# Output weights gated, summed and split beside the first attention units instead of in the output stage

## The chip, the core and the metric

The kernel runs on one core of one Trainium2 chip. The metric is the device time of one execution in microseconds, as a median over several runs. The engines are TensorE (PE, matmuls; PEld is its weight load), VectorE (DVE), ScalarE (ACT), GpSimd (POOL) and SyncE (SP), which here issues nearly all of the DMAs. Each engine works through its own instructions in order. On-chip memory is SBUF; matmuls write to PSUM; DRAM is reached by DMA.

## The reference

One layer of a hybrid backbone: 2048 latent tokens and 256 context tokens of width 1024. After a modulated RMS norm, one input projection feeds a bidirectional gated delta-rule scan (branch A, 4 heads) and a windowed grouped-query attention (branch B, 8 heads of 64, window 128, all context keys, a sink). Both go through their own projections and are merged by gates, then comes the output projection with a gated residual:

```python
def _merge(ya, yb, ga, gb, w_proj_a, w_proj_b, w_out):
    y = jax.nn.sigmoid(ga) * (ya @ w_proj_a) + jax.nn.sigmoid(gb) * (yb @ w_proj_b)
    return y @ w_out
...
    x = x + gate[:, None] * _merge(ya, yb, ga, gb, w_proj_a, w_proj_b, w_out)
```

`gate` is one vector of 1024 numbers, a factor for each output column, known early in the kernel. All data is fp32.

## The kernel before

**Numbers.** Each fp32 operand of a large matmul is split into a high half (a cast to a rounded fp32 format) and a low half (the rest), and each product is three matmuls: high by high, high by low, low by high. The cast is mostly on ACT, the subtraction for the low half on DVE or POOL.

**Stages.** The modulation and the norm; the input projection; the delta-rule scan over chunks; attention in 32 units (16 blocks of 128 tokens, 2 key heads); the two branch projections with the merge (`project`, lines 1280 to 1310); the output stage (from line 1372). A scheduler orders the first stages. It lets TensorE run gate products of the input projection (24 matmuls each, `rps`, lines 586 to 588) and later the projections' matmuls (`pps`, lines 1293 to 1295) between those of the scan and of the attention units, as fillers. The tokens are in four groups `gi` of 512, worked in the order 1, 2, 0, 3.

**Attention.** A unit has four heads' scores (`sc`, lines 971 to 974), their maximum and exponential (`pr`, DVE line 978, ACT line 980), a scaling (POOL line 988), transposes on TensorE (`pt`, line 1002), the split of the transposed probabilities (`ph` on ACT, line 1004, and `pl` on DVE, line 1006) and the products with the values (`av`, lines 1008 and 1009). `avt` then carries the result to DRAM (ACT line 1012, DVE line 1013, POOL line 1014, a DMA). Scores are two units ahead of the products. Twelve filler matmuls stand in most of the first units.

**Merge.** For group `gi` and column block `m` of 128, `project` loads the gates `ta` and `tb`, multiplies both projections by them, adds them on DVE or POOL and stores the sum to the DRAM tensor `ysp`. The last group's column blocks 6 and 7 are summed late, inside the output stage (`late_sum`, lines 1312 to 1324).

**Output stage.** The product of each 256 tokens by 1024 columns is made by seven block products instead of eight (Strassen-Winograd), `u` = 0 to 7 being the 256-token units. On the weights' side there are the blocks B11, B21, B22 and the sums T3 = B22 - B12, T2 = T3 + B11, T1 = B22 - T2, T4 = B21 - T2; on the activations' side A11, A12, A22, S1 to S4. One block product is 12 matmuls of 128x512 (line 1539 high by high, 1540 with the weights' low half, 1541 with the activations' low half `al`). The order of the products: each of the first two units' seven in pairs (P1 of u=0 and u=1, P2 of both, P3, P7, P6, P5, P4), then unit by unit. The four blocks of `w_out` are loaded from ACT's queue (line 1394) during the last group's projection and split there and in the first products: casts on ACT, the low halves and sums as 128x2048 instructions on DVE and POOL (lines 1411, 1444, 1446, 1578, 1583). The activations are read from `ysp` (line 1406). `his` (ACT, line 1421) and `los` (DVE, POOL for P4, line 1425) split them, five and four products ahead. `store` (lines 1489 to 1494) multiplies each finished quadrant by `gate` (line 1491), adds the residual's `x` (line 1492) and sends it out. The order of DVE, ACT, POOL and TensorE in this stage is written out by hand.

## Time and profile before

| | |
|---|---|
| time, median of 3 runs | 1974.95 us (1970.47 to 1976.83) |
| profiled execution | 1977.22 us |
| its span | 1975.5 us |
| granted TensorE clock, mean | 0.994 |
| busy: PE / DVE / ACT / POOL | 96% / 77% / 41% / 35% |

The profile is of one execution. A row of a timeline has its start, its duration, the engine with the line of the kernel, the operation, and the tiles written and read; in brackets stands how long the engine was idle before, and what ended that. A row of groups ends with the count, the busy time, the mean duration in ns and the idle time before. "SPq" is a DMA issue on SyncE, and its duration is that of the issue. Line numbers in the rows are those of the kernel before.

### The profile page before, as it was taken

To read this page: it belongs to the slowest core of one execution; us is meant where nothing else is said; L and a number is where in the kernel's file an instruction comes from. 1 tells how busy PE (TensorE), PEld (TensorE's weight loads), DVE (VectorE), ACT (ScalarE), POOL (GpSimd) and SP (SyncE) were. 2 spreads that over 40 slices of the span, in tenths; PEclk is the share of its full clock that TensorE was granted. 3 is DMA by queue.
4 is the path that set the end of the run, shared out by engine and by line. 5 is a ranking of instruction groups with operands and counts; after the bars stand their busy time and mean duration, and the time that the engine had idled before them with its cause. 6 is when DMAs were issued, how large, how long until landed. Compare 5 with 4: busy or idle time off the path is not lost. (4 is left out here: it accounts for less than half of the span.)

```text
span 1975.5 us, 32093 instructions
## 1 busy us (share of the span) xinstructions
PE 1902.6 (96%) x10931; PEld 1596.3 (81%) x10931; DVE 1512.4 (77%) x2873; ACT 815.6 (41%) x2011; POOL 701.3 (35%) x772
## 2 busy tenths in 40 slices
PE   6899999989999899999999999999999999999998
PEld 3888888788998787887888888888878887877786
DVE  7888766678776899999778776535787868757888
ACT  6865545544443322211122233324765646532321
POOL 2652111235543201104222334323555443422675
PEclk9999999999999999999999999999999999999999
DMA  7453226765546633537887777765455645355453
GB/s 267 161 154 93 87 89 161 190 166 166 152 146 169 178 108 115 151 96 208 230 251 219 224 227 228 197 182 188 136 182 178 195 150 173 113 190 175 144 171 134
DMA packets 387640, 333.13 MB, mean 169 GB/s; under 512 B 83928, under 2 KB 307472, under 8 KB 386836
## 3 DMA queue, kind: packets, MB, share of 16 engines
q1 hardware_dynamic: 352132, 288.58, 50.4%
q10 hardware_dynamic: 35344, 42.49, 6.2%
q8 instruction: 87, 1.43, 0.3%
q14 instruction: 77, 0.63, 0.1%
HBM read 220.28 MB, written 109.13 MB: 167 GB/s over the span
## 5 line engine op out<-in xcount | busy, mean ns | idle before, releaser
L586 PE MATMUL rps<-hh,wh 128*128 128x512 f32 x768 | 308.5, 402 | 6.5 <-DVE rt L880 5.4
L588 PE MATMUL rps<-hh,wl 128*128 128x512 f32 x768 | 307.7, 401 | 0.2 <-DVE wl L244 0.2
L587 PE MATMUL rps<-hl,wh 128*128 128x512 f32 x768 | 306.3, 399 | 0.0
L625 DVE SCALAR_TENSOR_TENSOR cacc<-y,cw,cacc 128x512 f32<-128x512 f32 (+1 forms) x224 | 163.5, 752 | 23.3 <-ACT cacc L623 21.0
L586 PEld LDWEIGHTS rps<-hh,wh 128*128 128x128 f32 x768 | 144.9, 189 | 41.8 <-DVE rt L880 6.3
L588 PE MATMUL lps<-hh,wl 128*128 128x512 f32 (+1 forms) x448 | 171.6, 383 | 1.7 <-DVE wl L244 1.7
L586 PE MATMUL lps<-hh,wh 128*128 128x512 f32 (+1 forms) x448 | 172.0, 384 | 0.8 <-POOL wh L243 0.6
L588 PEld LDWEIGHTS rps<-hh,wl 128*128 128x128 f32 x768 | 144.8, 188 | 32.6 <-DVE wl L244 0.3
L587 PEld LDWEIGHTS rps<-hl,wh 128*128 128x128 f32 x768 | 144.8, 189 | 32.5
L587 PE MATMUL lps<-hl,wh 128*128 128x512 f32 (+1 forms) x448 | 171.0, 382 | 0.0
L1006 DVE TENSOR_TENSOR pl<-pt,ph 128x512 fp32r<-128x512 f32 x156 | 105.6, 686 | 42.3 <-ACT ph L1004 41.4
L1004 ACT CAST ph<-pt 128x512 fp32r<-128x512 f32 x156 | 90.8, 585 | 107.8 <-PE pt L1002 72.8
L878 ACT ACTIVATE rt<-rps 128x512 f32<-128x512 f32 x96 | 57.2, 596 | 181.5 <-PE rps L588 157.9
L978 DVE CUSTOM_DVE_ANT_0 pr<-sc,band,sk 128x640 f32<-128x640 f32 (+1 forms) x128 | 106.7, 862 | 19.8 <-PE sc L974 12.1
L988 POOL TENSOR_SCALAR pr<-pr,sm 128x640 f32<-128x640 f32 (+1 forms) x128 | 101.4, 813 | 54.7 <-DVE sm L986 39.9
L809 DVE TENSOR_TENSOR btmp<-N 128x62 f32<-128x62 f32 (+30 forms) x124 | 117.4, 946 | 3.1
L811 DVE TENSOR_TENSOR N<-N,btmp 128x62 f32<-128x62 f32 (+30 forms) x124 | 116.1, 936 | 3.0
L980 ACT ACTIVATE pr<-pr,sm 128x640 f32<-128x640 f32 (+1 forms) x128 | 104.1, 815 | 24.1 <-DVE sm L978 24.1
L1293 PE MATMUL pps<-yh,wph 128*128 128x512 f32 x256 | 105.7, 415 | 2.4 <-DVE tb L1304 2.1
L244 DVE TENSOR_TENSOR wl<-wr,wh 128x512 fp32r<-128x512 f32 x120 | 91.6, 775 | 20.2 <-POOL wh L243 17.9
L243 POOL TENSOR_SCALAR wh<-wr 128x512 fp32r<-128x512 f32 x72 | 49.5, 700 | 156.4 <-PE lps L587 85.2
L1295 PE MATMUL pps<-yh,wpl 128*128 128x512 f32 x256 | 101.6, 398 | 0.9 <-POOL wpl L1255 0.9
(382 smaller groups left out, 5028.2 us busy)
## 6 DMA issues: line engine op xcount, KB each, us to landing
wr<-in_w_in_dram SPq DMA_DIRECT2D x120, 256.0 KB
kw<-Ksp SPq DMA_DIRECT2D x28, 384.0 KB
x<-vsp SPq DMA_DIRECT2D x36, 256.0 KB
k<-ksp SPq DMA_DIRECT2D x34, 256.0 KB
kT<-kTsp SPq DMA_DIRECT2D x34, 256.0 KB
wm<-in_w_mod_dram SPq DMA_DIRECT2D x16, 512.0 KB
xt<-in_x_dram SPq DMA_DIRECT2D x16, 512.0 KB
dtl<-Dsp SPq DMA_DIRECT2D x32, 256.0 KB
```

What stands on the lines that cost most here:

```text
L586: T.matmul(ps, lhsT=wh[:, k], rhs=xh[:, k], start=k == 0, stop=False)
L587: T.matmul(ps, lhsT=wh[:, k], rhs=xl[:, k], start=False, stop=False)
L588: T.matmul(ps, lhsT=wl[:, k], rhs=xh[:, k], start=False, stop=k == kt - 1)
L625: V.scalar_tensor_tensor(a, y[:, t:t + n], cw[:, m, t:t + 1], a, op0=ALU.mult, op1=ALU.add)
L809: V.tensor_tensor(tv, A[:, m + 1:, m].unsqueeze(2).to_broadcast([h1 + n, r, m]), A[:, m, 0:m].unsqueeze(1).to_broadcast([h1 + n, r, m]), o ...
L811: V.tensor_tensor(A[:, m + 1:, 0:m], A[:, m + 1:, 0:m], tv, op=ALU.add)
L978: V.tensor_tensor_reduce(s_, ps[:, o:768], band[:, b0:b0 + W + 256], -0.125, sk[:, 1, hd:hd + 1], ALU.add, ALU.min, sm[:, h, 1:2])
L980: S.activation(s_, s_, AF.Exp, scale=-1.0, bias=sm[:, h, 1:2], accum_out=sm[:, h, 2:3])
L988: G.tensor_scalar(p[:, h, :W + 256], p[:, h, :W + 256], sm[:, h, 3:4], 1.0, op0=ALU.mult, op1=ALU.mult)
L1006: V.tensor_tensor(pl, pt, f32(ph), op=ALU.subtract)
L1293: T.matmul(ps, lhsT=wh[:, k, ms], rhs=hs[k], start=k == 0, stop=False)
L1295: T.matmul(ps, lhsT=wl[:, k, ms], rhs=hs[k], start=False, stop=k == 3)
```

## The change

The blocks of `w_out` leave the output stage. A generator, `out_weights`, works on them in sixteen pieces of 128x512: for each quarter `k` of the rows it loads the four blocks' pieces, multiplies them by the columns of `gate` (on DVE for k = 0 and 1, on POOL for 2 and 3), forms the four sums on POOL, casts all seven to the high half on ACT, subtracts for the low half on DVE, and stores both halves to one of seven new DRAM tensors `wsp` (0.5 MB a store, 28 stores). It has seven steps for each quarter. The first two quarters are called ahead of unit 0's products, the last two by two steps after each unit, and their instructions are placed behind the unit's last ones on ACT, DVE, POOL and SP. Pieces (`wb`) and halves (`whl`) have two buffers each.

The output stage then loads the seven finished matrices, high and low halves together (2.1 MB each, `load_w`), and no longer touches weights. The loads stand in SP's queue: three of them between the last group's gate loads, four behind the last of these, between loads of `x`. Since the gate is in the weights, `store` only adds: `gather` adds a product, straight from PSUM where it can, to the `x` tile. There are ten `x` tiles instead of four. `ysp` is laid out so that 128 tokens of all columns lie together, and one DMA reads both column halves (`yA1`, `yA2`). The gate's broadcast tile in the output stage is gone.

```diff
-    ysp = many("ysp", 4, [128, KT, 512])
+    ysp = many("ysp", 4, [4, 128, KT, 128])
+    wsp = {nm: dscr(f"w{nm}", [128, 2, 4, 512]) for nm in ("B11", "B21", "B22", "T3", "T2", "T1", "T4")}
...
+    def out_weights(pool):
+        gates_ = [pool.tile([128, 512], F32, name="gbc", tag="tb") for _ in range(2)]
+        for j, t in enumerate(gates_):
+            dma(t, gsp[:, j * 512:j * 512 + 512].to_broadcast([128, 512]))
+        for k in range(4):
+            b = {}
+            for pair in (("B22", "B12"), ("B11", "B21")):
+                t = pool.tile([128, 2, 512], F32, name="wb", tag="ybh")
+                for n, nm in enumerate(pair):
+                    i, j = int(nm[1]) - 1, int(nm[2]) - 1
+                    b[nm] = t[:, n]
+                    dma(b[nm], ins["w_out"][0, i * 512 + k * 128:i * 512 + k * 128 + 128, j * 512:j * 512 + 512])
+            yield
+            def gated(nm):
+                (V if k < 2 else G).tensor_tensor(b[nm], b[nm], gates_[int(nm[2]) - 1], op=ALU.mult)
+            def put(nm, src):
+                t = pool.tile([128, 2, 512], F32R, name="whl", tag="ybl")
+                S.copy(t[:, 0], b[src])
+                V.tensor_tensor(t[:, 1], b[src], f32(t[:, 0]), op=ALU.subtract)
+                dma(wsp[nm][:, :, k], f32(t))
+            gated("B22")
+            gated("B12")
+            put("B22", "B22")
+            yield
+            G.tensor_tensor(b["B12"], b["B22"], b["B12"], op=ALU.subtract)
+            gated("B11")
+            put("T3", "B12")
+            yield
...
+            G.tensor_tensor(b["B21"], b["B21"], b["B11"], op=ALU.subtract)
+            put("T1", "B22")
+            put("T4", "B21")
+            yield
...
+        for _ in range(14):
+            next(beside)
         for i, (n, kv) in enumerate(units):
             if i + AHEAD < len(units):
                 start(i + AHEAD)
-            weighted(n, kv, qs[n], pr.pop(i))
+            ended = weighted(n, kv, qs[n], pr.pop(i))
+            with ExitStack() as paced_by:
+                for e in ended:
+                    paced_by.enter_context(tc.issue_after(e.ins))
+                next(beside, None)
+                next(beside, None)
...
+            dma(ysp[gi][:, :, m].rearrange("o p c -> p o c"), us[0].rearrange("p (o c) -> p o c", c=128))
...
         def load_w(nm):
-            i, j = int(nm[1]) - 1, int(nm[2]) - 1
-            adma(B[nm], ins["w_out"][0, i * 512:i * 512 + 512, j * 512:j * 512 + 512].rearrange("(k p) c -> p k c", p=128))
+            t = home.get(nm, hr).tile([128, 2, 4, 512], F32R, name=nm)
+            dma(f32(t), wsp[nm])
+            hi[nm], lo[nm] = t[:, 0], t[:, 1]
...
+            for m, jobs in enumerate(([(load_w, "B11")], [(load_quad, 0, "A1"), (load_quad, 1, "A1")], [(load_w, "B21")],
+                                      [(load_quad, 0, "A2"), (load_quad, 1, "A2")], [(load_w, "B22")])):
+                with tc.issue_after(last["t", m].ins):
+                    for f, *a in jobs:
+                        f(*a)
...
-                S.copy(hi["B11"], B["B11"])
-                split_lo("B11", V)
...
-                S.copy(hi["B22"], B["B22"])
-                V.tensor_tensor(B["B12"], B["B22"], B["B12"], op=ALU.subtract)
...
-            split_lo("B22", G)
-            split_lo("T3", G, "B12")
...
-        def store(u, q, t, eng):
-            xr, dst, gate, j = X.pop((u, q))
-            eng.tensor_tensor(t, t, gate, op=ALU.mult)
-            (V if u == 7 else G).tensor_tensor(xr, t, xr, op=ALU.add)
+        def gather(eng, u, q, t):
+            xr = X[u, q][0]
+            eng.tensor_tensor(xr, t, xr, op=ALU.add)
+        def store(u, q, ps):
+            gather(V, u, q, ps)
+            xr, dst, j = X[u, q]
             dma(dst, xr)
-            load_x(j + 4)
+            load_x(j + 10)
...
             elif nm == "P5":
-                h2 = wq.tile([128, 2, 512], F32, name="hold2", tag="wl")
-                V.tensor_tensor(h2[:, 0], ps, held[u][:, 0], op=ALU.add)
-                V.tensor_tensor(h2[:, 1], ps, held[u][:, 1], op=ALU.add)
-                V.tensor_tensor(h2[:, 0], R[u, "P3"], h2[:, 0], op=ALU.add)
-                store(u, "11", h2[:, 1], V)
-                store(u, "01", h2[:, 0], V)
...
+                store(u, "11", ps)
+                store(u, "01", ps)
             elif nm == "P4":
-                V.tensor_tensor(held[u][:, 1], ps, held[u][:, 1], op=ALU.add)
-                store(u, "10", held[u][:, 1], gp)
+                store(u, "10", ps)
...
+                for j in range(2):
+                    load_x(j)
+                load_w("T3")
+                for j in range(2, 6):
+                    load_x(j)
+                load_w("T2")
+                load_w("T1")
+                for j in range(6, 10):
+                    load_x(j)
+                load_w("T4")
```

How the instructions stand. First SP's queue at the scan's end, where the first attention units' loads are issued. `sza` and `yasp` are the scan's last gated outputs, `wr` the weights of the gate products, `kw`, `kc`, `qT` and `vw` the attention's loads. Before:

```order
L239 DMA wr<-in_w_in_dram 128x4x128 x2
L1125 DMA yasp_138<-sza 128x4x128
L956 DMA kw<-Ksp 128x2x384 x4
L1125 DMA yasp_135<-sza 128x4x128
L239 DMA wr<-in_w_in_dram 128x4x128 x2
L929 DMA kc<-Ksp 128x2x256 x2
L931 DMA vc<-Vsp 128x2x256
```

And now:

```order
L948 DMA gbc<-gsp 128x512 x2
L956 DMA wb<-in_w_out_dram 128x512 x4
L966 DMA wB_137<-whl 256x1x512
L240 DMA wr<-in_w_in_dram 128x4x128
L1179 DMA yasp_142<-sza 128x4x128
L240 DMA wr<-in_w_in_dram 128x4x128
L966 DMA wT_138<-whl 256x1x512
L966 DMA wB_135<-whl 256x1x512
L930 DMA kc<-Ksp 128x2x256 x2
L932 DMA vc<-Vsp 128x2x256
```

The pieces' loads and three of their stores now stand ahead of the attention's first loads, and two more stand behind these.

Second, DVE's line from the scan's end to the first scores, after the change (`L960` multiplies by the gate, `L965` makes a low half, `L1025` is line 978 before). Before, the instructions of lines 960 and 965 are not there:

```order
L1262 TENSOR_TENSOR oa_13330<-ops,oa_13330 128x512
L960 TENSOR_TENSOR wb<-wb,gbc 128x512
L1170 TENSOR_TENSOR oa_13330<-oa_13330,fss 128x512
L960 TENSOR_TENSOR wb<-wb,gbc 128x512
L965 TENSOR_TENSOR whl<-wb,whl 128x512
L960 TENSOR_TENSOR wb<-wb,gbc 128x512
L245 TENSOR_TENSOR wl<-wr,wh 128x512
L1178 SCALAR_TENSOR_TENSOR sza<-fps,gw,sza 128x512
L960 TENSOR_TENSOR wb<-wb,gbc 128x512
L245 TENSOR_TENSOR wl<-wr,wh 128x512
L965 TENSOR_TENSOR whl<-wb,whl 128x512 x4
```

Two more of the first quarter's low halves stand behind the first two scores' maxima, and the second quarter's eleven instructions between these and unit 0's end. The last two quarters' fourteen low halves are spread over units 1 to 7, two behind each unit's `avt` or a little later.

Third, SP's queue from the end of the last group's gate loads (`ta`, `tb`) to the first stores of output, after the change. Before, the weights' loads stood in ACT's queue instead, four of 1 MB:

```order
L1375 DMA ta<-gasp_126 128x512
L1513 DMA xr<-in_x_dram 128x512 x2
L1443 DMA T_19662<-wT_138 128x4096
L1513 DMA xr<-in_x_dram 128x512 x4
L1443 DMA T_19672<-wT_139 128x4096
L1443 DMA T_19674<-wT_140 128x4096
L1513 DMA xr<-in_x_dram 128x512 x4
L1443 DMA T_19684<-wT_141 128x4096
L1380 DMA ysp_134<-ta 128x4x128 x2
L1523 DMA out_dram<-xr 128x512 x2
```

The last four matrices now wait in this queue behind everything that the merge loads, and the last two `ysp` stores and the first output stores wait behind them.

More of the change, by code (lines that the diff above doesn't have):

```diff
@@ L1308, in project @@
                 continue
-            (V if gi == 3 else G).tensor_tensor(us[0], us[0], us[1], op=ALU.add)
-            dma(ysp[gi][:, m], us[0])
+            last["sum"] = (V if gi == 3 else G).tensor_tensor(us[0], us[0], us[1], op=ALU.add)
+            dma(ysp[gi][:, :, m].rearrange("o p c -> p o c"), us[0].rearrange("p (o c) -> p o c", c=128))
         return left
+    late_loads = []
     def late_sum(gi, m, us):
@@ L1330, in _hybrid @@
     psum_phase("right", sc=2, pt=2, av=1)
+    pj_ = tc.tile_pool(name="proj", bufs=2, side="right", reuse_waits="tile")
+    pj = pj_.__enter__()
     al_ = tc.tile_pool(name="attl", bufs=2, reuse_waits="tile")
@@ L1334, in _hybrid @@
     ar = ar_.__enter__()
-    attention(al, ar, [4 * gi + j for gi in (1, 2, 0, 3) for j in range(4)], att_consts(al))
+    attention(al, ar, [4 * gi + j for gi in (1, 2, 0, 3) for j in range(4)], att_consts(al), out_weights(pj))
     gates(list(range(BESIDE, 22)), (1, 0))
     wp, last = {}, {}
-    with tc.tile_pool(name="proj", bufs=2, reuse_waits="tile") as pj:
+    if True:
         raw = [pj.tile([128, 2, 512], F32, name="wpr", tag=tag) for tag in ("ybh", "ybl")]
@@ L1473, in s1 @@
             Y[u, "S1"] = Y[u, "A11"]
-        R, held, early = {}, {}, {}
+        with tc.high_priority(tc.cur_priority - p_last), \
+                tc.manual_schedule(engines={EN.DVE, EN.Activation, EN.Pool}):
+            for m, jobs in enumerate(([(load_w, "B11")], [(load_quad, 0, "A1"), (load_quad, 1, "A1")], [(load_w, "B21")],
[3 more added lines that the diff above has]
+                        f(*a)
+            with tc.issue_after(last["yh", 3].ins), tc.issue_after(last["yl", 3].ins):
+                for k in range(2):
+                    his(k)
+                    los(k)
+                s3(0, V)
+                s2(0, V)
+                s3(1, V)
+                s2(1, V)
+        for k in range(2, NP):
+            pair(k)
+        R, held = {}, {}
         outs = [(u, q) for u, nm in seq for q in {"P2": ["00"], "P5": ["11", "01"], "P4": ["10"]}.get(nm, [])]
@@ L1502, in outputs @@
                 S.copy(held[u][:, 0], ps)
+                gather(G, u, "00", held[u][:, 0])
             elif nm == "P2":
-                og = ev.tile([128, 512], F32, name="og", tag="rt")
-                V.tensor_tensor(og, ps, held[u][:, 0], op=ALU.add)
-                if u < 2:
-                    early[u] = og, G
-                else:
-                    store(u, "00", og, gp)
+                store(u, "00", ps)
+            elif nm == "P3":
+                gather(V, u, "01", ps)
             elif nm == "P6":
@@ L1540, in product @@
                 T.matmul(ps, lhsT=h[:, j], rhs=wl[:, j], start=False, stop=False)
-                end = T.matmul(ps, lhsT=l[:, j], rhs=wh[:, j], start=False, stop=j == 3)
-            return end
+                T.matmul(ps, lhsT=l[:, j], rhs=wh[:, j], start=False, stop=j == 3)
         with tc.manual_schedule(engines={EN.DVE, EN.Activation, EN.Pool, EN.PE}):
@@ L1610, in _hybrid @@
                 if k < len(seq):
-                    end = product(k)
-                if k == 3:
-                    with tc.issue_after(end.ins):
-                        dma(gbc, gsp.to_broadcast([128, D]))
-                        for j in range(4):
-                            load_x(j)
+                    product(k)
                 if k:
```

142 lines of the change are left out of this document (47 added, 95 removed).

## The prediction

> **What bounds the kernel now.** I read the page's busy shares first, then the chain, then the table by stretches, then TensorE's waits in the stretches that the change touches.
>
> ```profile
> span 1975.5 us, 32093 instructions
> PE 1902.6 (96%) x10931; PEld 1596.3 (81%) x10931; DVE 1512.4 (77%) x2873; ACT 815.6 (41%) x2011; POOL 701.3 (35%) x772
> DVE 0%; issue 0%
> ```
>
> TensorE is busy 96% of the span, so only its 73 us without work, and work that it does slowly, can be won. The chain of waits is no help: it holds five pieces at the very end. So each stage is read by itself.
>
> ```profile
> 1801.00:1875.00 74.00, 65.98 (x274) 51.64 (x273) 65.86 (x63) 20.21 (x30) 40.42 (x22) 0.98 0.46 143
> 1875.00:1968.00 93.00, 92.88 (x402) 74.94 (x400) 79.59 (x89) 19.29 (x35) 65.44 (x41) 1.00 0.48 156
> 1300.00:1350.00 50.00, 49.06 (x233) 40.05 (x233) 15.39 (x32) 10.98 (x32) 9.52 (x19) 1.00 0.75 231
> 1350.00:1400.00 50.00, 49.92 (x281) 42.91 (x280) 35.96 (x84) 30.70 (x69) 21.34 (x27) 1.00 0.44 140
> 1400.00:1450.00 50.00, 49.02 (x273) 40.35 (x272) 39.89 (x87) 37.19 (x79) 26.08 (x28) 1.00 0.49 150
> ```
>
> Columns: stretch, its length, then busy time of PE, PEld, DVE, ACT and POOL, granted clock, DMA share, GB/s. The output products run from 1801 to 1968. Their second part is dense: 402 matmuls in 93.00 us, 0.2313 us each. At that pace the 274 of the first part need 63.4 us; they took 74.0. So 10.6 us are lost there, and in the second part none. The attention's opening units (1350 to 1450) have TensorE full, with DVE free for 14.0 and 10.1 us of 50.
>
> TensorE's waits between 1801 and 1875 name the loser:
>
> ```profile
> PE P L1541 <- DVE al L1425: 7.3, 4, 3.1
> PE P L1541 <- POOL al L1425: 0.7, 1, 0.7
> ```
>
> Total, times, longest. All are waits for `al`, the low half of an activation. Why it is late, by the timelines of DVE, POOL and PE:
>
> ```profile
> 1798.45 2.29 DVE L1411 TENSOR_TENSOR B21l<-B,B21h 128x2048 fp32r<-128x2048 f32 x1 [1.99 <-PE pps L1294]
> 1800.66 9.76 DVE L1425 TENSOR_TENSOR al<-yA,ah 128x512 fp32r<-128x512 f32 x1
> 1812.26 0.68 DVE L1425 TENSOR_TENSOR al<-yA,ah 128x512 fp32r<-128x512 f32 x1
> ...
> 1798.71 6.59 POOL L1411 TENSOR_TENSOR B22l<-B,B22h 128x2048 fp32r<-128x2048 f32 x1 [41.01 <-PE pps L1295]
> 1805.26 4.61 POOL L1411 TENSOR_TENSOR T3l<-B,B12h 128x2048 fp32r<-128x2048 f32 x1
> ...
> 1810.48 0.50 PE L1541 MATMUL P<-B21h,al 128*128 128x512 f32 x1 [3.10 <-DVE al L1425]
> 1812.02 0.63 PE L1539 MATMUL P<-B21h,ah 128*128 128x512 f32 x1
> 1812.45 0.63 PE L1540 MATMUL P<-B21l,ah 128*128 128x512 f32 x1
> ...
> 1833.55 0.50 PE L1541 MATMUL P<-T2h,al 128*128 128x512 f32 x1 [1.56 <-DVE al L1425]
> ```
>
> A 0.68 us subtraction took 9.76 us while POOL split two weight matrices; it ended with them. TensorE stood 3.10 us, and afterwards ran for a while at 0.43 us a matmul (1812.02 to 1812.45), which is why 8.0 us of waits cost 10.6. The other stalls have the weights' wide DVE instructions ahead of them in line, 2.29 us each (first row).
>
> **The change part by part.**
>
> *Output stage.* It takes all weight work off this stage: both POOL splits, DVE's nine 2.29 us instructions (20.6 us), ACT's seven wide casts, and the gate's multiplications. DVE's 65.86 us in the first part fall by about 9.1 (the stretched subtraction) and five to six wide ones, to 45 of 74. What remains there is work like that of the second part, where TensorE loses nothing. I take 10 of the 10.6 us; at least 6 should go, since the 3.10 us stall with its slow matmuls and the 1.56 us one both stand directly behind such work.
>
> *The end.*
>
> ```profile
> 1967.48 0.40 PE L1541 MATMUL P<-T4h,al 128*128 128x512 f32 x1
> 1971.81 0.69 DVE L1527 TENSOR_TENSOR xr<-hold,xr 128x512 f32<-128x512 f32 x1
> 1972.53 0.33 SPq L1528 DMA_DIRECT2D out_dram<-xr  x1
> ```
>
> From the last matmul's start to the span's end there are 8.0 us, in which DVE works off its line. Now one addition straight from PSUM follows the last product: 0.40 + 0.69 + about 0.2 of handing over + the last store's 2.97 (1972.53 to 1975.5) is 4.3. Gain 3.5, between 3 and 4.
>
> *Loads of the split weights.* High and low halves in fp32 are 2.1 MB a matrix, against 1.05 MB and only four matrices before. In SP's line the last four wait behind the final project loads:
>
> ```profile
> 1798.96 0.90 SPq L1318 DMA_DIRECT2D tb<-gbsp  x2
> ...
> 1801.21 0.39 PE L1539 MATMUL P<-B11h,ah 128*128 128x512 f32 x1
> ```
>
> These were out by 1799.86. From there: 1.05 MB of those loads, ten input rows of 0.26 MB and four matrices, 12.05 MB. The first product starts at 1801.21; at 2.8 us for each (12 matmuls), T4's, the thirteenth, starts at 1834.8. That asks for 345 GB/s. The traffic view of 1763 to 1782, where the weights come in today:
>
> ```profile
> GB/s 362 78 0 0 69 52 198 392 405 410 401 375 342 317 303 309 381 384 375 401 401 367 371 375 388 388 388 392 375 388 388 379 348 341 346 396 401 406 392 276
> DMA packets 4366, 6.20 MB, mean 327 GB/s; under 512 B 192, under 2 KB 1728, under 8 KB 4365
> ```
>
> At its mean of 327 the last weights are 1.9 us late; at 303, the lowest slice of the busy part, 5; at 375 or more, not at all. I take 2, bounds 0 and 5. For the earlier three matrices I add nothing: the 51 us from 1750 to 1801 moved this,
>
> ```profile
> DMA packets 7736, 11.82 MB, mean 232 GB/s; under 512 B 536, under 2 KB 2449, under 8 KB 7735
> ```
>
> and must now move some 15 MB (2.1 more of weights, 1.3 more of activations), which is 299 GB/s. The Trainium skill gives, in "DMA: Bandwidth & Descriptors", section Specifications, about 358 GB/s as a core's share of HBM; this trace has slices up to 410, so the measurement decides, and by the page's figure as an estimate this term would be 0 instead of 2.
>
> *The weight work's new place.* Sixteen pieces are multiplied (eight on DVE, eight on POOL), 16 sums on POOL, 28 casts on ACT, 28 subtractions on DVE, 28 stores of 0.5 MB. The nearest rows, by groups, 1350 to 1450:
>
> ```profile
> L244 DVE TENSOR_TENSOR wl<-wr,wh 128x512 fp32r<-128x512 f32 x4 | 3.2, 827 | 0.1
> L1275 DVE TENSOR_TENSOR yl<-yr,yh 128x512 fp32r<-128x512 f32 x2 | 1.3, 689 | 0.0
> L1004 ACT CAST ph<-pt 128x512 fp32r<-128x512 f32 x41 | 23.6, 584 | 15.9 <-PE pt L1002 10.1 <-PE av L1008 5.4
> L1255 POOL TENSOR_TENSOR wpl<-wpr,wph 128x512 fp32r<-128x512 f32 x4 | 5.1, 1289 | 2.4 <-ACT wph L1254 2.4
> ```
>
> So DVE gets 36 x 0.69 = 25 us, ACT 28 x 0.58 = 16, POOL 24 x 1.29 = 31. By the order of the instructions, of DVE's 36 the eleven of the first quarter stand at the scan's end and the first scores. They fit: DVE is idle 34.6 us of 1300 to 1350, and what they delay there (the last `sza` and the gate's splits) has fillers before it. Next:
>
> (a) The first scores come one gate product later on TensorE, and that product's boundary loses its cover. Such a boundary today:
>
> ```profile
> 1331.91 0.50 PE L586 MATMUL rps<-hh,wh 128*128 128x512 f32 x1 [0.69 <-ACT rt L878]
> ```
>
> With the slower matmul behind it, 1 us.
>
> (b) The second quarter's eleven stand between unit 0's scores and its end, in some 22 us (1350 to 1372) with 28% of DVE free, 6.2 us. They need 7.6: 1.4 late. If each of the four POOL sums beside them also holds one up by its 1.29, 5.2 more. Bounds 0 (DVE was free before 1350) and 7; I take 3, since DVE is handed these by a store's end too (two buffers only).
>
> (c) The last two quarters add two DVE, two ACT and 2.3 POOL instructions to each of units 1 to 7. The units' ends on DVE:
>
> ```profile
> 1372.91 0.68 DVE L1013 TENSOR_TENSOR avt<-av,avt 64x512 f32<-64x512 f32 x1
> ...
> 1449.88 0.68 DVE L1013 TENSOR_TENSOR avt<-av,avt 64x512 f32<-64x512 f32 x1
> ```
>
> Seven units lie between, 11.0 us each; DVE's 10.1 free of 50 are 2.2 a unit, against 1.4 needed. That fits, barely; ACT (37.19 of 50, plus 5.6) and POOL (26.08, plus 14) fit too. If each of the two meets a POOL instruction for its full 1.29, 4.0 stand against 2.2, and each unit ends 1.8 later: 13. TensorE has nothing else to do then, as the fillers are placed by units. Between 0 and 13 the nearest row is L244, a subtraction beside POOL's work that rose only from 0.69 to 0.83; that fits into the free time. I take 2 for queueing.
>
> The stores put qT, kw and szb loads behind themselves in SP's line; these are ahead by two units, 22 us, against some 3 for a store: nothing, unless the units themselves slip. The first projection's weights move behind the last pieces; gate products stand in front of them: nothing, up to 4.
>
> The sum: -10 - 3.5 + 2 + 1 + 3 + 2 = -5.5. From the profiled execution (1977.22, 1.7 around its span) that is 1971.7; it lay 2.3 above the median of the runs shown, from which it is 1969.5. I predict 1970.
>
> **The rivals.**
>
> *A, the opening hides everything.* DVE's idle 34.6 us ahead of 1350 take so much that units 0 to 7 lose nothing but (a), and the loads hold 375 GB/s: -13.5 + 1, 1962.5. For it: free time on all three engines. Against it: DVE's line is in order, and what is free is free in scraps.
>
> *B, slower: DVE's line in the opening units.* Place: from unit 0's `pl` to unit 7's. Price: POOL's long instructions hold each of DVE's added ones as the 9.76 us row was held: 1 + 6 + 12, with 2 for the loads, against 13.5: +7.5, 1982.5. It decides from the point at which a unit's added DVE time passes 2.2 us, that is, when its two instructions are held 0.4 us each on average, as by one POOL instruction in three. The Trainium skill says in "SBUF — State Buffer", section Who interferes with whom, that a DVE instruction with two SBUF inputs and a GpSimd instruction that reads SBUF hold each other for the whole instruction, while a DVE instruction with at most one SBUF input isn't held outside the two-port modes. All 36 added ones have two; attention's `pl` reads PSUM and isn't held itself. By that rule B would be the forecast; the 9.76 us row agrees with it. Against B: L244's 827 ns beside POOL's instructions.
>
> *C, no change: the loads.* T3 to T4 and the fourth matrix come at 303 GB/s and in turn: 5 and again some 3 at the third or sixth product, and the opening's 6: -13.5 + 14, 1975.5. The wait by `al` becomes a wait by a load. For it: twice the bytes. Against it: slices of 375 to 410.
>
> **How the numbers follow.** A measurement of this kernel can tell about 0.3%, 5.9 us, from no change: faster is below 1969.0, slower above 1980.9. Forecast 0.42, its own range 1965 to 1975, half of it faster; A 0.20, all faster; B 0.22, of which 0.18 slower; C 0.16, of which 0.05 slower. That is faster 0.21 + 0.20 = 0.41, slower 0.23, the same 0.36. A's and B's outer halves left out, the range is 1962 to 1984.
>
> **What would show it.** Right: no wait for `al` over 1 us between the first product and the second part, the first 274 output matmuls within 66 us; one DVE addition behind the last matmul and 4.3 us to the end; DVE's subtractions of the pieces near 0.7 to 0.9 us; the opening units ending 6 us late against the scan. For B: those subtractions at 1.3 us and above, and TensorE waiting for `ph`, `pl` or scores in units 0 to 7. For C: TensorE or ACT waiting for a DMA of T2, T1 or T4. Wrong altogether: if the scan or the gates' products ahead of the attention lose time, or if the stalls between 1801 and 1875 stay although the weight work is gone.

## The result, and the profile after

The changed kernel takes 2001.49 us (median of 6 runs, 1995.14 to 2005.34) where the kernel before takes 1975.37 beside it: 1.0132 of it, 95% interval 1.0112 to 1.0153. It is 26 us slower, and outside the range that was given. Its profiled execution has a span of 2003.0 us.

The page of the kernel after, its first lines:

```profile
span 2003.0 us, 32226 instructions
PE 1913.3 (96%) x10931; PEld 1607.0 (80%) x10931; DVE 1489.6 (74%) x2880; ACT 819.4 (41%) x2032; POOL 698.3 (35%) x781
```

TensorE has the same 10931 matmuls, and they occupy it 11 us longer. Of these, 3 us lie ahead of the scan's end; the others are slower matmuls around the waits (granted clock 0.95 up to unit 0's end and 0.98 from there to unit 7's, 1.00 in both before). The rest of the 27.5 us is waiting. To place them I read four moments in each kernel's timelines: the last transposes of the scan (`fps` on PE), the ends of unit 0 and unit 7 (`avt` on DVE), the first output product and the last matmul (`P` on PE). All are starts of rows. In us:

| | scan's end to unit 0 | unit 0 to 7 | scan's end to first output product | first to last output matmul | last matmul's start to the end |
|---|---|---|---|---|---|
| before | 48.4 | 77.0 | 476.7 | 166.3 | 8.0 |
| after | 63.7 | 87.9 | 502.4 | 167.8 | 4.1 |

So 25.7 us are lost between the scan's end and the first output product, the output stage gains nothing (1.5 us more), and the end gains 3.9. The remaining 4.2 us lie ahead of the scan's end; that moment stood between 1324.0 and 1332.9 in the executions of all the kernels below, and I draw nothing from it.

**The opening.** First unit 0. ACT's and DVE's waits from 1328 to 1392 in the kernel after (total, times, longest):

```profile
ACT whl L964 <- DMA wT<-whl: 9.8, 3, 4.7
ACT whl L964 <- DMA wB<-whl: 2.7, 2, 1.4
DVE whl L965 <- ACT whl L964: 13.5, 5, 5.3
```

ACT's cast waits until the store of two casts earlier has left its buffer, and DVE stands in line behind that cast. One such case by the timelines of SP, ACT, DVE and PE:

```profile
1345.10 0.53 SPq L966 DMA_DIRECT2D wT<-whl  x1
...
1354.10 0.62 ACT L964 CAST whl<-wb 128x512 fp32r<-128x512 f32 x1 [4.15 <-DMA wT<-whl]
...
1354.75 0.69 DVE L965 TENSOR_TENSOR whl<-wb,whl 128x512 fp32r<-128x512 f32 x1 [2.50 <-ACT whl L964]
1359.17 0.69 DVE L965 TENSOR_TENSOR whl<-wb,whl 128x512 fp32r<-128x512 f32 x1 [3.72 <-ACT whl L964]
1359.78 0.88 DVE L1025 CUSTOM_DVE_ANT_0 pr<-sc,band,sk 128x640 f32<-128x640 f32 x1
...
1360.72 0.44 PE L1018 MATMUL sc<-kw,qT 128*128 128x384 f32 x1 [2.85 <-DVE sm L1025]
```

A store issued at 1345.10 had not released its buffer before 1354.10, nine us later. The scores' maximum (L1025) stands behind two low halves, and TensorE waits 2.85 us for it. The second of these low halves waited 3.72 us for a cast that stood on ACT behind an exponential (L1027, 1357.71), so stores are not all of it.

Then the later units. First the stretches 1392 to 1467 of the kernel after and 1373 to 1450 of the kernel before (columns as in the prediction), then groups on DVE in them:

```profile
1392.00:1467.00 75.00, 64.66 (x349) 53.41 (x349) 70.10 (x122) 51.07 (x110) 56.44 (x52) 0.97 0.75 243
...
L965 DVE TENSOR_TENSOR whl<-wb,whl 128x512 fp32r<-128x512 f32 x12 | 13.7, 1153 | 1.9 <-ACT whl L964 1.2 <-DMA vw<-Vsp 0.6
L1029 DVE TENSOR_TENSOR es<-sm,sk 128x4 f32<-128x4 f32 x6 | 8.1, 1345 | 0.0
L1031 DVE TENSOR_TENSOR es<-es,sm 128x4 f32<-128x4 f32 x6 | 3.5, 575 | 0.2 <-ACT es L1030 0.2
L1032 DVE TENSOR_SCALAR es<-es 128x4 f32<-128x4 f32 x6 | 2.5, 414 | 0.2
```

```profile
1373.00:1450.00 77.00, 75.94 (x422) 63.07 (x422) 60.58 (x134) 54.70 (x118) 38.00 (x41) 1.00 0.51 157
L982 DVE TENSOR_TENSOR es<-sm,sk 128x4 f32<-128x4 f32 x7 | 3.5, 496 | 0.0
L984 DVE TENSOR_TENSOR es<-es,sm 128x4 f32<-128x4 f32 x7 | 1.8, 264 | 1.4 <-ACT es L983 1.4
L985 DVE TENSOR_SCALAR es<-es 128x4 f32<-128x4 f32 x7 | 1.2, 169 | 0.2
```

DVE is busy 93% instead of 79%, while TensorE does 349 matmuls in 75 us instead of 422 in 77. A low half takes 1153 ns on average, not 689, and the sum of four numbers a partition, on which the softmax waits, 1345 instead of 496; the two instructions behind that sum (L1031, L1032) are slower too. The averages mix two kinds: of the 15 low halves between the ends of unit 0 and unit 7, nine took 0.67 to 0.69 us and six 1.10 to 3.71. What holds those shows where DVE's and POOL's timelines are laid side by side:

```profile
1406.44 3.71 DVE L965 TENSOR_TENSOR whl<-wb,whl 128x512 fp32r<-128x512 f32 x1 [0.64 <-DMA vw<-Vsp]
...
1405.84 1.28 POOL L1061 TENSOR_TENSOR avt<-avt,szb 64x512 f32<-64x512 f32 x1 [1.12 <-DVE pl L1053]
1407.08 1.28 POOL L960 TENSOR_TENSOR wb<-wb,gbc 128x512 f32<-128x512 f32 x1
1408.33 1.27 POOL L972 TENSOR_TENSOR wb<-wb 128x512 f32<-128x512 f32 x1
```

The low half ends 0.55 us behind the end of POOL's row of three (1410.15 and 1409.60). The first of the three is attention's own, the other two are weight work. The five other slow ones overlap weight work twice and attention's scaling of the probabilities (L1035) three times. TensorE's waits in the whole kernel fit this:

```profile
PE av L1056 <- DVE pl L1053: 10.4, 13, 2.1
PE sc L1018 <- DVE sm L1025: 7.5, 6, 2.8
PE P L1556 <- DMA T<-wT: 4.9, 3, 1.8
PE P L1558 <- DVE al L1465: 2.4, 2, 2.1
```

The first two were 0.9 and 2.5 us before.

**The output stage.** The waits for `al` have shrunk from 7.3 to 2.4 us, and waits for the loaded matrices (4.9) stand in their place. Its first part by stretches, and rows from the timelines of DVE and SP:

```profile
1831.00:1905.00 74.00, 64.67 (x263) 50.76 (x262) 44.77 (x61) 14.72 (x26) 26.59 (x18) 0.95 0.82 302
...
1833.51 0.69 DVE L1359 SCALAR_TENSOR_TENSOR ta<-ta,pps 128x512 f32<-128x512 f32 x1 [5.84 <-DMA ta<-gasp]
...
1841.97 0.32 SPq L1375 DMA_DIRECT2D ta<-gasp  x1
```

```profile
1843.00:1875.00 32.00, 27.13 (x115) 21.44 (x114) 14.01 (x21) 6.25 (x11) 9.14 (x7) 0.99 1.00 391
```

DVE fell from 65.86 to 44.77 us, as forecast, and it did not help: the transfer engines are at 82%, 302 GB/s. Before, the last gate loads were out 1.3 us ahead of the first output product (1799.86 against 1801.21). Now the last one is issued 10.9 us behind it (1841.97 against 1831.08), because the gate loads share the queue and the transfers with 2.1 MB matrices (DVE waits 5.84 us for one), and T3 to T4 stand behind it. A gate load waits in SP's queue until an earlier `ysp` store has left its buffer: 22.4 us of such waits (L1357) from 1770 to 1850, where the kernel before has 7.8 from 1740 to 1802 (L1303). Once the matrices are issued, the transfers run at 391 GB/s (1843 to 1875).

**The end** is as forecast: one addition behind the last matmul, 4.1 us to the end.

```profile
1998.91 0.39 PE L1558 MATMUL P<-T,al 128*128 128x512 f32 x1
1999.34 0.69 DVE L1518 TENSOR_TENSOR xr<-P,xr 128x512 f32<-128x512 f32 x1 [0.93 <-PE P L1558]
```

### The profile page after: what moved, and what is told of

It reads as the page before. It is cut to its first block, busy times and chain, and to the rows that moved or that the text cites. A ratio compares the mean times of both kernels' runs of the same rounds, so it can differ in the third digit from the quotient of the medians.

```text
span 2003.0 us, 32226 instructions
## 1 busy us (share of the span) xinstructions
PE 1913.3 (96%) x10931; PEld 1607.0 (80%) x10931; DVE 1489.6 (74%) x2880; ACT 819.4 (41%) x2032; POOL 698.3 (35%) x781
## 5 line engine op out<-in xcount | busy, mean ns | idle before, releaser
L1025 DVE CUSTOM_DVE_ANT_0 pr<-sc,band,sk 128x640 f32<-128x640 f32 (+1 forms) x128 | 106.7, 862 | 13.1 <-PE sc L1021 8.2
L1035 POOL TENSOR_SCALAR pr<-pr,sm 128x640 f32<-128x640 f32 (+1 forms) x128 | 103.5, 827 | 34.9 <-DVE sm L1033 18.7
L1027 ACT ACTIVATE pr<-pr,sm 128x640 f32<-128x640 f32 (+1 forms) x128 | 104.0, 815 | 14.5 <-DVE sm L1025 10.4
L244 POOL TENSOR_SCALAR wh<-wr 128x512 fp32r<-128x512 f32 x72 | 51.2, 724 | 163.6 <-PE lps L588 85.5
```

The costliest lines, as they stand in the source:

```text
L1025: V.tensor_tensor_reduce(s_, ps[:, o:768], band[:, b0:b0 + W + 256], -0.125, sk[:, 1, hd:hd + 1], ALU.add, ALU.min, sm[:, h, 1:2])
L1027: S.activation(s_, s_, AF.Exp, scale=-1.0, bias=sm[:, h, 1:2], accum_out=sm[:, h, 2:3])
L1035: G.tensor_scalar(p[:, h, :W + 256], p[:, h, :W + 256], sm[:, h, 3:4], 1.0, op0=ALU.mult, op1=ALU.mult)
```

## The experiments

The table gives the same five stretches for each run; "opening" is the scan's end to the first output product. The ratios are to the kernel before on the same chip. A row's stretches are those of one execution: the two executions of run 9's kernel differ by 1.6 us to unit 0 and 1.5 in the opening, so differences of that size say nothing.

| run | to unit 0 | unit 0 to 7 | opening | output stage | ratio, 95% interval |
|---|---|---|---|---|---|
| before | 48.4 | 77.0 | 476.7 | 166.3 | 1 |
| after | 63.7 | 87.9 | 502.4 | 167.8 | 1.0132 (1.0112 to 1.0153) |
| 1 no weight work | 54.2 | 73.6 | 476.7 | 168.8 | 1.0001 (0.9990 to 1.0013) |
| 2 small stores | 61.1 | 83.4 | 491.4 | 168.3 | 1.0085 (1.0061 to 1.0109) |
| 3 traffic only | 62.8 | 74.9 | 485.2 | 168.0 | 1.0052 (1.0035 to 1.0069) |
| 4 before, POOL's splits in pieces | 48.4 | 77.1 | 474.5 | 165.4 | 1.0005 (0.9989 to 1.0020) |
| 5 as 2, no POOL work | 60.6 | 80.5 | 491.5 | 167.2 | 1.0064 (1.0043 to 1.0085) |
| 6 as 2, no low halves | 57.8 | 77.6 | 484.5 | 167.6 | 1.0035 (1.0021 to 1.0050) |
| 7 as 1, half the bytes | 55.4 | 73.6 | 478.3 | 153.5 | 0.9933 (0.9911 to 0.9954) |
| 8 before, splits on DVE | 48.4 | 76.5 | 475.5 | 171.2 | 1.0031 (1.0017 to 1.0045) |
| 9 splits in the output stage | 56.8 | 79.4 | 488.6 | 155.9 | 0.9979 (0.9965 to 0.9993) |
| 9 again | 58.4 | 79.5 | 487.1 | 155.5 | 1.0004 (0.9994 to 1.0015) |
| 10 as 9, gating on DVE | 58.4 | 80.4 | 485.6 | 155.1 | 1.0003 (0.9987 to 1.0019) |
| 11 as 3, behind the loads | 55.0 | 79.2 | 483.9 | 168.6 | 1.0038 (1.0022 to 1.0053) |
| 12 as 9, behind the loads | 56.5 | 78.4 | 488.6 | 153.5 | 0.9966 (0.9952 to 0.9981) |

### 1. No weight work

```diff
     def out_weights(pool):
+        ... (one tile of two pieces is loaded and stored four times to a spare tensor `wfull`)
+        yield
+        return
...
-            dma(f32(t), wsp[nm])
+            dma(f32(t), wfull)
```

> Edit: the changed kernel without any work on the weights beside attention (no gating, sums, splits and piece stores; the output stage loads one 2.1 MB matrix of other values seven times, with the same bytes and queue). If the 27 us that the changed kernel loses between the scan's end and the first output product all come from the weight work beside the first units, that stretch is as long as before and the time is about 1975 (2001.5 - 27). If the moved loads, the new pool or the order of the attention's loads have a part in it, more than 1980. The output stage is untouched by this edit: its waits for the loads (4.9 us in the changed kernel) stay, and 1831 to 1999 remains some 167 us long.

The opening is 476.7 us, to the tenth that of before, and the ratio is 1.0001. So the whole loss of the opening is the weight work. Unit 0 ends 5.8 us later, since the first scores come a gate product later, and unit 7 has caught up with part of that (127.8 against 125.4), the first output product with all: the lost cover of the product's boundary costs nothing in the end. Against this run the weight work costs 9.5 us up to unit 0's end, 14.3 in units 1 to 7, and 1.9 after them. And the output stage without any weight arithmetic in it is no faster than before.

### 2 and 3. Small stores; traffic only

```diff
-                dma(wsp[nm][:, :, k], f32(t))
+                dma(wsp[nm][0:8, :, k], f32(t[0:8]))
... (the output stage loads `wfull`, as in run 1)
```

> Edit: all computation on the weights kept, but each piece's store sends 8 of 128 partitions (a sixteenth of the bytes), and the output stage loads one other matrix seven times. Theory of the store round trip (two buffers, each cast waits for the store two casts earlier, and that store waits behind the attention's own loads): ACT's waits for stores of pieces fall from 12.5 us before unit 0's end to 3 or less, unit 0 ends some 10 us earlier, time about 1990 if units 1 to 7 are bound by DVE, 1980 if these too wait for stores. Theory of DVE's line (time of its added instructions and POOL holding them): unit 0 gains 3 or less and units 1 to 7 still lose 1.8 each, time 1997 or more.

```diff
             def gated(nm):
-                (V if k < 2 else G).tensor_tensor(b[nm], b[nm], gates_[int(nm[2]) - 1], op=ALU.mult)
+                pass
             def put(nm, src):
-                t = pool.tile([128, 2, 512], F32R, name="whl", tag="ybl")
-                S.copy(t[:, 0], b[src])
-                V.tensor_tensor(t[:, 1], b[src], f32(t[:, 0]), op=ALU.subtract)
-                dma(wsp[nm][:, :, k], f32(t))
+                for x in range(2):
+                    dma(wsp[nm][:, x, k], b[src])
... (and the four sums on POOL are gone)
```

> Edit: the pieces are loaded and stored as in the changed kernel, same bytes (raw values in place of both halves), but nothing is computed on them: no gating, sums, casts or subtractions. Theory of DVE's line: units 1 to 7 take 11.0 us each again as before, and the opening's loss falls from 27 to 8 or less, time 1982 or less. Theory of traffic alone (the attention's loads late behind 18.9 MB of pieces): the loss stays above 15, time 1990 or more.

The opening loses 14.7 us with the computation and a sixteenth of the store bytes, 8.5 with the traffic and no computation; together 23.2 of the 25.7. So neither theory has it alone. But the two do not simply add up to the changed kernel. In run 3 the first scores come 30.2 us after the scan's end, 21.1 in the changed kernel, 19.8 in runs 1 and 2: its 8.6 us at unit 0 are a delay that the changed kernel does not have. Beside the computation, the store bytes are worth the difference between the changed kernel and run 2, 11.0 us. The store round trip was worth less than expected at unit 0: up to there ACT's waits for stores fell from 12.5 to 4.4 us and DVE's for casts from 13.5 to 6.0, and unit 0 ends only 2.6 us earlier, not 10. Units 1 to 7 keep 9.8 of their 14.3 us with small stores, and lose 1.3 with traffic alone: there it is mostly the computation.

### 5 and 6. Whose computation

```diff
... (run 5, on run 2: the four sums on POOL are gone)
-                (V if k < 2 else G).tensor_tensor(b[nm], b[nm], gates_[int(nm[2]) - 1], op=ALU.mult)
+                if k < 2:
+                    V.tensor_tensor(b[nm], b[nm], gates_[int(nm[2]) - 1], op=ALU.mult)
```

> Edit: as the run with small stores, and POOL's part of the weight work is left out too (the 16 sums and the gating of the last two quarters); DVE's 36 and ACT's 28 instructions stay. In the run with small stores units 1 to 7 took 83.4 us against 73.6 without weight work, 9.8 more. If POOL's instructions are what stretches DVE's line (each holding a DVE instruction with two SBUF inputs), that falls to 3 or less and the added low halves take about 0.7 to 0.9 us each. If DVE's own added time is the cause, it stays at 7 or more.

```diff
... (run 6, on run 2)
-                V.tensor_tensor(t[:, 1], b[src], f32(t[:, 0]), op=ALU.subtract)
-                dma(wsp[nm][0:8, :, k], f32(t[0:8]))
+                dma(wsp[nm][0:8, 0:1, k], f32(t[0:8, 0:1]))
```

> Edit: as the run with small stores, but DVE's 28 subtractions for the low halves are left out (only high halves are stored); POOL's 24 instructions and ACT's 28 stay. If DVE's added time is the cause of the 9.8 us in units 1 to 7, it falls to 3 or less. If POOL's occupation alone (its scaling of the probabilities then comes later) is the cause, it stays at 7 or more. Both may be needed together: then this and the run without POOL's part each fall below 5.

Without POOL's 24 instructions the opening loses as much as with them (14.8), though units 1 to 7 lose 6.9 us instead of 9.8. Without DVE's 28 low halves the opening loses 7.8, units 1 to 7 4.0. So the low halves on DVE cost about half. Leaving POOL's weight work out freed the softmax's small sums (148 ns on average, 716 in run 2), but not the low halves: 1075 ns from 1396 to 1470 of run 5, where those of run 2 took 803 between the ends of unit 0 and unit 7. One case of run 5 on DVE and POOL:

```profile
L973 DVE TENSOR_TENSOR whl<-wb,whl 128x512 fp32r<-128x512 f32 x14 | 14.9, 1075 | 3.4 <-ACT whl L972 3.4
...
1447.24 0.67 DVE L973 TENSOR_TENSOR whl<-wb,whl 128x512 fp32r<-128x512 f32 x1
1447.91 1.79 DVE L973 TENSOR_TENSOR whl<-wb,whl 128x512 fp32r<-128x512 f32 x1
...
1447.39 1.76 POOL L1065 TENSOR_TENSOR avt<-avt,szb 64x512 f32<-64x512 f32 x1 [3.47 <-DVE avt L1064]
```

Here it is attention's own instruction on POOL that holds the second low half. Of the 14 in units 1 to 7 of this run, five took 1.78 to 1.79 us, all beside that multiplication of `avt`, and nine 0.67 to 0.69. They stand behind a unit's `avt` on DVE, and POOL then multiplies that `avt`.

What the units lose follows DVE's busy time between the ends of unit 0 and unit 7:

| run | DVE busy | length |
|---|---|---|
| 1 no weight work | 57.8 | 73.6 |
| 3 traffic only | 59.2 | 74.9 |
| 6 no low halves | 64.8 | 77.6 |
| 5 no POOL work | 68.0 | 80.5 |
| 2 small stores | 75.6 | 83.4 |
| after | 82.4 | 87.9 |

Each us added to DVE goes with some 0.6 us of length in the last four rows, from the first 7 us on, although DVE has 15.8 us free in run 1. Runs 9, 10 and 12 are near that (69.7, 70.6 and 65.5 us busy in 79.4, 80.4 and 78.4). The kernel before (60.6 in 77.0) and run 11 (61.4 in 79.2) can't be set beside these rows, since TensorE does 423 matmuls there instead of 403 to 413. That the added time itself is the cause, and not what else these runs add (casts on ACT, work on POOL), is argued from the order of the rows; no run adds DVE time alone.

### 4 and 8. The kernel before, without POOL's long splits

```diff
... (run 4)
-            eng.tensor_tensor(lo[nm], B[src or nm], f32(hi[nm]), op=ALU.subtract)
+            for j in (range(4) if eng is G else (slice(0, 4),)):
+                eng.tensor_tensor(lo[nm][:, j], B[src or nm][:, j], f32(hi[nm])[:, j], op=ALU.subtract)
```

> Edit: the kernel before, with POOL's two 128x2048 splits (6.59 and 4.61 us) cut into four 128x512 instructions each. If POOL's long instructions are what held the activations' subtraction for 9.76 us, that subtraction takes 3 us or less, the 3.10 us wait is gone and its slow matmuls with it: 3 to 5 us faster than before, about 1971. If DVE's line is simply too full there, the wait stays above 2 us and the time within 1 us of before.

```diff
... (run 8: split_lo("B22", V) at k == 0, split_lo("T3", V, "B12") at k == 1)
-            split_lo("B22", G)
-            split_lo("T3", G, "B12")
```

> Edit: the kernel before, with the two wide splits taken from POOL and put into DVE's line (2.29 us each) behind the low halves that the next products need; nothing runs on POOL there. Cutting them into pieces on POOL had changed nothing, as POOL's pieces followed one another without a gap and held another DVE instruction (4.14 us for a 0.69 us addition). If that holding is the cause of the waits for the low halves, the first wait (3.10 us) and most of the others go, and the kernel is 5 to 8 us faster than before, 0.996 or 0.997 of it. If DVE's line is simply full there, as 36 us of work in 36 us would have it, the waits only move to later products: within 2 us of before.

Run 4: the subtraction that had taken 9.76 us takes 1.80, and the time is the same (1.0005). POOL's pieces come without a gap between them, and the next addition on DVE is held for 4.14 us. Run 8 takes both splits off POOL, and is slower. None of DVE's rows there is held now, and both engines wait for activations (ACT, then DVE; the third row is ACT in the kernel before):

```profile
1812.92 0.62 ACT L1421 CAST ah<-yA 128x512 fp32r<-128x512 f32 x1 [9.50 <-DMA yA<-ysp]
...
1818.12 0.69 DVE L1460 TENSOR_TENSOR yA<-yA,yA 128x512 f32<-128x512 f32 x1 [3.85 <-DMA yA<-ysp]
...
1810.43 0.62 ACT L1421 CAST ah<-yA 128x512 fp32r<-128x512 f32 x1 [11.43 <-DMA yA<-ysp]
```

In run 8 the first output product started at 1805.62. In the kernel before, the held subtraction ended at 1810.42, and ACT had waited for the activations until 1810.43. So behind the held subtraction stood a second limit at the same time, the activations' loads: the 10.6 us that I had given to the weight work were not its alone.

### 7. Half the bytes

```diff
... (on run 1)
-            dma(f32(t), wfull)
-            hi[nm], lo[nm] = t[:, 0], t[:, 1]
+            dma(f32(t[:, 0]), wfull[:, 0])
+            hi[nm], lo[nm] = t[:, 0], t[:, 0]
```

> Edit: as the run without weight work, and the output stage loads only the high half of each matrix (1.05 MB instead of 2.1 MB) and uses it in place of the low half too; products, activations and outputs unchanged. If the loads' bytes are what eats the output stage's gain, the waits for T3, T2 and T4 (6.9 us there) go, the stretch from the first to the last output product falls from 168.8 to about 159, and the time is 8 to 10 us below that run: 0.995 of before. If the queue's order (behind the last gate loads) is the cause whatever the bytes, the stretch stays above 165.

The output stage takes 153.5 us, 15.3 less than in run 1, and TensorE has no wait in it (from 1807 to 1881):

```profile
1807.00:1881.00 74.00, 74.00 (x325) 60.79 (x325) 48.83 (x66) 18.92 (x32) 32.86 (x23) 1.00 0.74 259
```

The queue's order is the same, so it is the bytes. The time of the last gate load's issue follows them: 10.5 to 12.3 us behind the first output product in the changed kernel and the runs with its bytes (1, 2, 3, 5, 6, 11), 1.2 to 4.3 us behind it in those with half (7, 9, 10, 12). The 14.3 us that the changed kernel needs more than run 7 are 9.3 us of waits (4.9 for the matrices, 4.2 for halves of activations) and 5.0 of slower matmuls. This is also what the output stage can give without a wait: 12.8 us against before, and 3.9 at the end.

### 9, 10 and the repeat. Store once, split in the output stage

```diff
             def put(nm, src):
-                t = pool.tile([128, 2, 512], F32R, name="whl", tag="ybl")
-                S.copy(t[:, 0], b[src])
-                V.tensor_tensor(t[:, 1], b[src], f32(t[:, 0]), op=ALU.subtract)
-                dma(wsp[nm][:, :, k], f32(t))
+                dma(wsp[nm][:, k], b[src])
...
+        def split(nm):
+            S.copy(hi[nm], f32(lo[nm]))
+            V.tensor_tensor(lo[nm], f32(lo[nm]), f32(hi[nm]), op=ALU.subtract)
... (split in the order of the products; the pieces take over the halves' buffers, and a quarter's
... steps stand in another order; run 10: all gating on DVE)
```

> Edit: the changed kernel, but only the gating and the sums stay beside attention; each gated matrix is stored and loaded once (1.05 MB instead of 2.1 MB), and the output stage makes its halves again, with seven casts on ACT and seven subtractions of 2.29 us on DVE, none on POOL. If the low halves on DVE and the bytes are what costs, as the runs so far have it: the opening loses 8 instead of 26 us (7.8 without the low halves), and the output stage, at half the bytes and with 16 us more on a DVE that was busy 45 of 74 us, takes 155 to 160 us from its first to its last product instead of 168, with the end 4 us shorter: 1972 to 1978 where before has 1978, a ratio of 0.997 to 1.000. If the gating and sums on POOL and the pieces' traffic suffice to delay the opening, it loses 15 or more and the ratio is 1.003 or above. If the output stage's DVE is too full with the splits, its products take over 163 us.

> Edit: as the run with the splits in the output stage, and the gating of the last two quarters on DVE too instead of POOL (eight multiplications of 0.69 us moved; POOL keeps the 16 sums). The opening loses 11.9 us there against the run without weight work, 5.8 of it in units 1 to 7. If POOL's instructions beside the units are what delays them (they hold DVE's small sums of the softmax), halving them takes 2 to 4 us off: ratio to before about 0.996. If the pieces' traffic and the queue's order are the cause, or DVE's own time, nothing changes or it is slower: 0.998 or more.

> Edit: the run with the splits in the output stage once more, beside the variant with all gating on DVE, so that both have the same chip. It should again be 0.996 to 0.999 of before (0.9979 the first time).

The output stage keeps its gain (155.9 and 155.5 us, 10 less than before) with seven wide subtractions back on DVE (2.29 us each for the blocks, 2.56 on average for the sums). The opening loses 11.9 and 10.4, more than the 8 expected. The intervals of the two timings, 0.9979 and 1.0004, do not meet, so this version is within about 0.2% of before. Moving the gating to DVE changed nothing that can be told from that.

### 11 and 12. The pieces behind the first units' loads

```diff
-        for _ in range(14):
-            next(beside)
+        with tc.issue_after(firsts[-1]):
+            for _ in range(14):
+                next(beside)
... (`firsts` holds the last load of each of the first two units)
```

> Edit: as the run with the pieces' traffic alone (nothing computed), but every load and store of pieces is put behind the second unit's... to be exact behind the last of the first two units' loads in the order, so that kc, qT, kw and vw no longer wait in SP's queue behind stores. That run lost 8.5 us between the scan's end and the first output product, all of it by unit 0's end, with the first scores 10.4 us later than without weight work. If the queue's order is the cause, the first scores come at about 20 us after the scan's last transposes (30 there) and the loss falls to 3 or less. If it is the traffic itself (18.9 MB beside the units' loads), the loss stays above 6, only later.

> Edit: the run with the splits in the output stage (gating and sums beside attention), with the pieces' loads and stores behind the first units' loads in the same way. It lost 11.9 us in the opening, 2.6 by unit 0's end and the rest later. If the queue's order is the larger part, the opening loses 6 or less and the ratio to before is 0.995 to 0.998. If the work of the sums, now later and beside units 0 and 1, is the larger part, the opening loses 10 or more, and the ratio stays at 0.998 to 1.001.

In run 11 the first scores come 14.1 us after the scan's end instead of 30.2, and still the opening loses 7.2 us instead of 8.5: of the 7.8 us won at unit 0 (55.0 instead of 62.8), 3.5 are left at unit 7 and 1.3 at the first output product. So SP's order is the smaller part and the traffic itself the larger. From 1340 to 1395, 40 slices and the totals:

```profile
GB/s 387 404 383 384 394 339 200 288 403 404 407 407 404 405 404 400 368 379 391 354 361 307 305 381 375 380 383 381 384 317 128 80 87 190 295 159 379 290 379 340
DMA packets 12517, 18.44 MB, mean 335 GB/s; under 512 B 1035, under 2 KB 6155, under 8 KB 12515
```

The same order in run 12 leaves the opening at 488.6 us and the output stage at 153.5, without a wait. At 0.9966 (0.9952 to 0.9981) it is the fastest kernel here that computes the reference: 0.34% under before and 1.6% under the change. That the order in the queue is what sets it apart from run 9 isn't shown: their intervals overlap, and its opening is no shorter in the profiled execution, which was the slowest of its twelve (1976.25, median 1969.40).

## Why the prediction was wrong

The forecast was 5.5 us faster, the result is 26 us slower. By the terms of its sum:

- **The end, -3.5:** right, -3.9.
- **The weight work off the output stage, -10:** the work did go (DVE 65.86 to 44.77 us), and run 7 shows 12.8 us behind it, but only where the loads are out of the way. The sign named for this, no wait for `al` over 1 us, was missed in the changed kernel (2.1) and met in run 7.
- **The loads, +2 (0 to 5):** this step failed. Against run 7's 153.5 us, the loads cost 14.3. The demand of 345 GB/s was worked out from the last gate loads being out at 1799.86, as before, and "for the earlier three matrices I add nothing". But the first three matrices delay these very gate loads: the last is issued 10.9 us behind the first product instead of 1.3 ahead of it, and the four last matrices stand behind it. The rate was not at fault: 391 GB/s from 1843 to 1875, above the 345 asked. The term was a bandwidth over a stretch whose start I took from the old kernel. The sign of rival C, waits for these matrices, came true (4.9 us).
- **(a) the lost cover, +1:** 0 by run 1.
- **(b) unit 0, +3 (0 to 7):** 9.5. This step failed too. The term was DVE's 1.4 us, put up to 3 for the buffers, with a store at 3 us; a store took nine, in traffic of 280 GB/s. But run 2 gives the store bytes only 2.6 of the 9.5, run 6 the low halves 3.3, run 5 POOL's work 0.5. The remaining 3.1 stay open; run 6 still has the loads, the multiplications and the casts.
- **(c) units 1 to 7, +2 (0 to 13):** 14.3. This step failed as well: "that fits into the free time". DVE's busy time between the two ends rose by 24.6 us (57.8 in run 1, 82.4), where fourteen low halves at 0.69 us are 9.7. The low halves took more, since six were held. The larger error is a term that was not there, attention's own small instructions: with POOL's added work beside them the softmax's three (L1029, L1031, L1032) took 17.2 us instead of the 6.4 of run 1. They took 13.3 without the low halves (run 6) and 3.5 without POOL's work (run 5). And free time did not absorb what did fit: run 6 adds 7.0 us, 1.0 a unit against 2.2 free, and loses 4.0. L244's 827 ns was not the wrong size by itself (803 in run 2), but a mean over low halves does not tell what POOL's rows do to other instructions.
- After unit 7, 1.9 that I had at nothing, hardly more than the scatter.

Together: -3.9 - 12.8 + 14.3 + 0 + 9.5 + 14.3 + 1.9 is 23.3, and the 4.2 us ahead of the scan's end make it the 27.5 between the two profiled spans.

So rival B was right in its place, and with 19 us near the 23.8 lost there. Its mechanism was half right: POOL's instructions held DVE's, but the added low halves stayed at 1.15 us on average, below its sign of 1.3, and more of the held time lay on attention's own small sums. What it lacked besides was the traffic. Of its rule, in the Trainium skill's "SBUF — State Buffer", section Who interferes with whom (a DVE instruction with two SBUF inputs and a GpSimd instruction that reads SBUF hold each other for the whole instruction), these traces agree: either side was held, for the two low halves from 1467.66 took 0.67 and 0.68 us in the changed kernel and POOL's multiplication beside them 2.29 instead of 1.28. They show one thing more: a DVE instruction can be held through several POOL instructions in a row (3.71 us through three, 1406.44). It also holds for attention's own instructions on POOL, so that leaving POOL's added work out (run 5) frees the softmax's sums and not the low halves. The rule had been weighed for DVE's added instructions, and not for those that attention already had.

And rival C came as well, at nearly twice the price that it had (14.3 instead of 8). I had given chances to B and C as if one excluded the other. They share the doubled bytes in part: 18.9 MB beside the opening and 14.7 MB in the output stage, though in the opening the computation loses 14.7 us even with small stores. The forecast took a value in the better half of each range where the rows bounding them were far apart, and all three ((b), (c) and the loads) came out past the worse end.

Of the reading of the kernel before, one part fell: the 3.10 us wait had been put down to POOL's splits alone. Runs 4 and 8 show that taking them away exposes the activations' loads.

## What to carry to other kernels

Work that is moved to "free" engine time through DRAM pays three times: in the line of the engine that takes it up, where free time absorbed only part of it here, in the traffic beside that stage, and in the loads where it returns. Count the bytes in both places, and start the second count from when the queue will be free in the new kernel, not in the old one. Store the smaller form and make the larger one again where an engine has time: one matrix and a split (run 9) took 12 us less in the output stage than two halves loaded. And price a moved instruction by the neighbours of its new place, in both directions: the 0.69 us subtractions took 1.15 us on average there, and the softmax's small instructions beside the moved POOL work 17.2 us instead of 6.4.

## What the runs showed of the hardware that was not expected

- Instructions on POOL that follow one another can hold a DVE instruction through all of them: 3.71 us for a 0.69 us subtraction beside three of 1.28. Cutting POOL's work into pieces (run 4) let one subtraction through after 1.80 us instead of 9.76, but a later addition was held for 4.14.
- Even four numbers a partition are held: the softmax's small sum took 1345 ns on average, 496 before, and 148 in run 5, where POOL has no weight work.
- A 0.5 MB store took nine us to release its buffer among the units' loads. With 18.44 MB in 55 us (335 GB/s, slices up to 407), a better order of the queue brought the first scores 16 us forward (run 11 against run 3), and the end of the opening only 1.3.
